# Moving a matmul's streamed weights 96 bytes into their buffers

## The chip, the cores and the metric

The kernel runs on one core of one Trainium2 chip. The metric is device time in microseconds (us) of one execution; lower is better. Before the change the median of three runs is 2471.81 us (2471.71 to 2472.35).

## The reference

The reference is a decoder trunk of two layers in float32, for one sequence of 256 tokens with 2,048 features. Cut to what matters here:

```python
u = rms_norm(h, mix_norm[0])
q, f, i, g = split(u @ w_a_in, 4)            # 2048 x 8192; i are the values
h = h + (norm(linear_attention(q, f, i)) * silu(g)) @ w_a_out
h = h + square(relu(rms_norm(h) @ w_mlp_up[0])) @ w_mlp_down[0]      # 2048 x 8192 x 2048
h = h + (p[0] @ w_ple_up[0]) * sigmoid(rms_norm(h) @ w_ple_gate[0])
k, v, f_logit = split(rms_norm(h) @ w_kvf)   # 2048 x (2048 + 2048 + 16)
dcum = cumsum(log_sigmoid(f_logit + b_f))
q = rms_norm(h, mix_norm[1]) @ w_b_q
h = h + softmax(q k^T / sqrt(128) + dcum_t - dcum_s, causal) v @ w_b_out
# then MLP and gate of layer 1, and a last rms_norm
```

## The kernel before, in words

**Splitting.** Every large product is made of float32r matmuls on split operands. A weight or an activation x becomes hi, its rounding to float32r, and lo = x - hi. A product is hi x hi + hi x lo + lo x hi, three matmuls that add up in PSUM.

**Loading weights.** `load_slab` (L79) loads a slab of up to 128 x 2,048 float32 weights by one DMA on SP's queue into `raw` (three buffers of 8,192 bytes a partition), or in parts. For each part (two as a rule) it takes a buffer `whi` and a buffer `wlo` of 1,024 elements (four buffers of each, in turn, 4,096 bytes a partition). ACT copies `raw` to `whi` (L93), DVE writes raw - whi to `wlo` (L94). So a slab fills two of the four buffers of each kind while the two before are in use.

**Feature-major products.** `mm_tile` (L98) makes 128 output features of all 256 tokens: for each of 16 chunks k of the input features, `mm_split` (L103) issues three matmuls (L112 to L114) whose stationary operand is a 128 x 128 block of `whi` or `wlo` and whose moving operand is 256 columns of the activation, `act[:, k, 0 or 1, :]`. Most of the kernel is made of these: the HGRN inputs, the output projections, both MLPs, the gates, keys and queries. The small products with `pt` (`ple`) take the same way.

**Token-major products.** `mm_tokens` (L118) makes 512 or 416 output features of all tokens, with tokens on the partitions. The roles are exchanged: the stationary operand is a 128 x 128 block of the activation, and the moving operand is the weight. Four slabs q hold four chunks of `cols` columns each. For each chunk and each half t of the tokens there are three matmuls (L131 to L133): activation hi x `whi`, activation hi x `wlo`, activation lo x `whi`. Thus one call has 4 x 4 x 2 x 3 = 96 matmuls. It is called four times with 512 columns for the values of layer 0 (`values`, one call before each fourth head, the first of them while x and the first weights are still being loaded, in smaller parts), and five times with 416 columns for the values and forget logits of layer 1 (the loop that fills `vv`).

**Where activations lie.** Split activations have a buffer of 16 x 2 x 256 elements and 64 more. `shifted` (L69) puts the data some elements into that buffer: 60 elements (240 bytes) in slots A and B, 28 (112 bytes) in slot C and for `pt`.

**Forget rows.** In the attention of layer 1, `cumulate` writes the negated running sums to `nd`, 16 x 256, and a DMA on POOL's queue stores them in a DRAM row buffer `dcum`. For each head `softmax` loads one row, broadcast to 128 partitions, into `ns` (two buffers, in turn), also on POOL's queue. `nd` has a buffer of its own.

**Order.** The order within each engine comes from the tile framework's scheduler and the program text. The framework places the buffers of a pool one after the other; the pool of `raw`, `whi` and `wlo` lies ahead of the pools that are opened later.

Of the kernel before, what the change touches and what calls it, by code (L numbers as in the profile page):

```python
# [10 lines left out]
F32 = mybir.dt.float32  # L11
F32R = mybir.dt.float32r
U32 = mybir.dt.uint32
AF = mybir.ActivationFunctionType
ALU = mybir.AluOpType
# [3 lines left out]
P = 128  # L19
T = 256  # L20
# [3 lines left out]
NH = 16  # L24
# [10 lines left out]
def yoco_kernel(ctx, tc, a, out):  # L35
    nc = tc.nc
    big = ctx.enter_context(tc.tile_pool(name="big", bufs=1))
    base = ctx.enter_context(tc.tile_pool(name="base", bufs=1))
    wp = ctx.enter_context(tc.tile_pool(name="wp", bufs=1))
# [36 lines left out]
        return shifted(big, KC, name, "slot" + which, 60)  # L76


    def load_slab(src, n, parts, before=None):  # L79

        raw = wp.tile([P, D], F32, name="raw", tag="raw", bufs=3)
        m = n // parts
        if not before:
            nc.sync.dma_start(raw[:, :n], src)
        got = []
        for i in range(parts):
            r = raw[:, i * m : (i + 1) * m]
            if before:
                before[i]()
                nc.sync.dma_start(r, src[:, i * m : (i + 1) * m])  # L90
            hi = wp.tile([P, 1024], F32R, name="whi", tag="whi", bufs=4)
            lo = wp.tile([P, 1024], F32R, name="wlo", tag="wlo", bufs=4)
            nc.scalar.copy(hi[:, :m], r)  # L93
            nc.vector.tensor_tensor(lo[:, :m], r, hi[:, :m].bitcast(F32), op=ALU.subtract)  # L94
            got.append((hi, lo))
        return got

# [3 lines left out]
    def mm_tile(src, act, kcs=KC):  # L101

        pairs = load_slab(src, kcs * P, 2 if kcs > 8 else 1)  # L103
        return mm_split(pairs, act, kcs)
# [12 lines left out]
    def mm_tokens(src, act, cols, before=None, after=None):  # L117

        pst = [psm.tile([P, 512], F32, name=f"pst{t}", tag="mm") for t in range(2)]
        for q in range(4):  # L120
            bef = before(q) if before else None
            parts = len(bef) if bef else 2
            pairs = load_slab(src(q), 4 * cols, parts, bef)
            for k in range(4):
                kk, m = 4 * q + k, 4 // parts
                hi, lo = (x[:, k % m * cols : (k % m + 1) * cols] for x in pairs[k // m])
                st, sp = kk == 0, kk == KC - 1
                for t in range(2):
                    o = pst[t][:, :cols]
                    tok = slice(t * P, (t + 1) * P)  # L130
                    nc.tensor.matmul(o, act[:, kk, 0, tok], hi, start=st, stop=False)  # L131
                    nc.tensor.matmul(o, act[:, kk, 0, tok], lo, start=False, stop=False)  # L132
                    nc.tensor.matmul(o, act[:, kk, 1, tok], hi, start=False, stop=sp)  # L133
            if after:
                after(q)
        return pst
# [96 lines left out]
    def ple(layer, u, stats, after, pool):  # L233

        praw = pool.tile([P, 2, T], F32, name="praw", tag="praw", bufs=1)
        nc.gpsimd.dma_start(praw, a["pT"][layer])
        pt = shifted(pool, 2, "pt", "pt", 28)
        for k in range(2):
            plain_split(pt, k, praw[:, k, :])
        rstd = None  # L240
        wu = None
        for n in range(KC):
            if n % 8 == 0:
                wu = load_slab(a["w_pu"][layer, n // 8], D, 2)
            pu = mm_split(wu, pt, kcs=2, off=2 * (n % 8))
            up = pool.tile([P, T], F32, name="up", tag="up", bufs=2)
            nc.scalar.copy(up, pu)
            last = layer == 1 and n == KC - 1
            ps = mm_tile(a["w_pg"][layer, n], u)
            rstd = rstd or stats.rstd()  # L250
            t = pool.tile([P, T], F32, name="gate", tag="gate", bufs=2)
            nc.vector.tensor_tensor(t, ps, rstd, op=ALU.mult)
            s = pool.tile([P, T], F32, name="sig", tag="sig", bufs=2)
            nc.scalar.activation(s, t, AF.Sigmoid)
            if last:

                nc.scalar.activation(scrap, s[:, 0:1], AF.Sqrt)
            nc.vector.tensor_tensor(up, up, s, op=ALU.mult)
            nc.vector.tensor_tensor(h[:, n, :], h[:, n, :], up, op=ALU.add)
            after(n)  # L260
# [18 lines left out]
    with tc.tile_pool(name="hg", bufs=2) as hp, tc.tile_pool(name="hps", bufs=1, space=PSUM) as hps:  # L279
# [60 lines left out]
        def values(grp):  # L340
            if grp == 0:
                return mm_tokens(lambda q: a["w_av"][0, q], u_a, 512,
                                 lambda q: [load_x(k, 1) for k in range(4)] if q == 0 else [load_x(4 * q), load_x(4 * q + 2)],
                                 lambda q: [stats.add(k) for k in range(4 * q, 4 * q + 4)])
            return mm_tokens(lambda q: a["w_av"][grp, q], u_a, 512)
# [226 lines left out]
    with tc.tile_pool(name="at", bufs=2) as ap, tc.tile_pool(name="aps", bufs=1, space=PSUM) as aps:  # L572
# [11 lines left out]
        for g in range(5):  # L584
            pv = mm_tokens(lambda q: a["w_vf"][g, q], u_kv, VC)
            if g == 0:
                norm["f"], norm["t"] = st_kv.rstd_both(aps, "pn")
            for t in range(2):
                nc.scalar.activation(vv[:, t, g * VC : (g + 1) * VC], pv[t][:, :VC], AF.Copy, scale=norm["t"][:, t : t + 1])
# [10 lines left out]
        nc.vector.tensor_scalar(ls, fl, 0.0, None, op0=ALU.min)  # L600
        nc.vector.tensor_tensor(ls, ls, fa, op=ALU.subtract)
        dt_ = ap.tile([P, 2, NH], F32, name="dt_", bufs=1)
        nd = ap.tile([NH, T], F32, name="nd", bufs=1)
        rows = dram.tile([NH, T], F32, name="dcum", tag="dcum")

        def cumulate():
# [169 lines left out]
```

## Time and profile before

| what | value |
|---|---|
| median of three runs | 2471.81 us |
| time of the profiled execution | 2472.09 us |
| its span, first to last instruction | 2470.0 us |
| mean granted TensorE clock | 0.998 |
| matmul records on PE | 20,808 |
| DVE busy, ACT busy | 1568.3 us, 1286.1 us |
| HBM read | 464.35 MB, 189 GB/s over the span |

How to read the profile: PE is the matmul engine, PEld its weight loads, DVE the vector engine, ACT the scalar engine, POOL the general one, SP the queue that issues the weight DMAs. A row such as "L112 PE MATMUL ps<-u_m,whi 128x256" names the line of the kernel, the engine, the output and the inputs, and the moving operand's shape. The length of a matmul in a row overlaps its neighbours, because matmuls are pipelined; the distance between the starts of two matmuls, in the timeline, is the pace. A float32 matmul that is not float32r appears as two records.

### The profile page before, as it was taken

The page shows a single profiled execution, that of the slowest core. Times are in us where ns is not written, and L with a number is a line of the kernel's source. Part 1 is how long each engine was busy: PE and PEld are TensorE (multiplying, and loading weights), DVE is VectorE, ACT ScalarE, POOL GpSimd, SP SyncE. Part 2 cuts the span into 40 slices and gives each one's busy share as a digit, 9 for nine tenths or more (in the row PEclk, how much of TensorE's full clock was granted, in tenths as well). Part 3 has the DMA queues.
Part 4 walks back from the last instruction along what each step waited for, and adds up shares of the span by engine and source line. Part 5 has one row for each costly group of instructions (what it writes and reads, how often), then busy time and mean ns, then how long its engine had stood idle before and what let it go on. Part 6 is the DMA issues. An engine that isn't in the chain of part 4 may idle for free.

```text
span 2470.0 us, 48653 instructions
## 1 busy us (share of the span) xinstructions
PE 2453.6 (99%) x20808; PEld 2431.0 (98%) x20808; DVE 1568.3 (63%) x2350; ACT 1286.1 (52%) x1966; POOL 23.1 (1%) x71
## 2 busy tenths in 40 slices
PE   9999999999999999999999999999999999999997
PEld 8999999999999999999999999999999999999997
DVE  8787797665555555556774566666555555555666
ACT  7666575555435435445664554555543443544564
POOL 1000000000000000000000000000000000000000
PEclk9999999999999999999999999999999999999999
DMA  7455445555555555555555655555555555555553
GB/s 256 172 180 181 184 167 203 201 189 190 201 190 192 201 188 194 199 188 195 197 179 185 198 180 171 181 196 188 195 198 189 197 196 190 197 194 190 199 192 120
DMA packets 68506, 469.62 MB, mean 190 GB/s; under 512 B 7937, under 2 KB 8641, under 8 KB 15041
## 3 DMA queue, kind: packets, MB, share of 16 engines
q1 hardware_dynamic: 66096, 460.88, 53.6%
q0 software_dynamic: 1760, 4.78, 1.0%
q8 instruction: 163, 2.67, 0.4%
q10 hardware_dynamic: 432, 0.85, 0.1%
q14 instruction: 55, 0.44, 0.0%
HBM read 464.35 MB, written 2.13 MB: 189 GB/s over the span
## 4 chain that ended last, share of the span: by engine, by line
PE 99%; DVE 0%; ACT 0%; DMA 0%; issue 0%; SPq 0%; DVEq 0%
PE ps L114 30%; PE ps L112 30%; PE ps L113 30%; PE pst L132 2%; PE pst L133 2%; PE pst L131 2%; PE pa L438 0%; PE pl L639 0%; PE ptp L662 0%; DMA h<-in_xT 0%; DVE h L709 0%; PE po L459 0%; PE ms L475 0%; PE pb L442 0%; PE pob L672 0%; PE pob L673 0%
## 5 line engine op out<-in xcount | busy, mean ns | idle before, releaser
L94 DVE TENSOR_TENSOR wlo<-raw,whi 128x1024 fp32r<-128x1024 f32 (+2 forms) x882 | 1069.2, 1213 | 674.2 <-ACT whi L93 673.4
L93 ACT CAST whi<-raw 128x1024 fp32r<-128x1024 f32 (+2 forms) x882 | 920.0, 1044 | 1083.4 <-PE ps L113 940.9
L112 PE MATMUL ps<-u_m,whi 128*128 128x256 f32 x2048 | 563.6, 275 | 0.0
L114 PE MATMUL ps<-u_m,wlo 128*128 128x256 f32 x2048 | 563.3, 275 | 0.0
L113 PE MATMUL ps<-u_m,whi 128*128 128x256 f32 x2048 | 563.3, 275 | 0.0
L112 PE MATMUL ps<-hid,whi 128*128 128x256 f32 x2048 | 563.2, 275 | 0.0
L113 PE MATMUL ps<-hid,whi 128*128 128x256 f32 x2048 | 563.2, 275 | 0.0
L114 PE MATMUL ps<-hid,wlo 128*128 128x256 f32 x2048 | 563.2, 275 | 0.0
L112 PEld LDWEIGHTS ps<-u_m,whi 128*128 128x128 f32 x2048 | 384.5, 188 | 0.1
L113 PEld LDWEIGHTS ps<-u_m,whi 128*128 128x128 f32 x2048 | 384.5, 188 | 0.1
L114 PEld LDWEIGHTS ps<-u_m,wlo 128*128 128x128 f32 x2048 | 384.4, 188 | 0.0
L112 PEld LDWEIGHTS ps<-hid,whi 128*128 128x128 f32 x2048 | 384.4, 188 | 0.0
L113 PEld LDWEIGHTS ps<-hid,whi 128*128 128x128 f32 x2048 | 384.4, 188 | 0.0
L114 PEld LDWEIGHTS ps<-hid,wlo 128*128 128x128 f32 x2048 | 384.4, 188 | 0.0
L112 PE MATMUL ps<-u_a,whi 128*128 128x256 f32 x768 | 214.0, 279 | 0.0
L114 PE MATMUL ps<-u_a,wlo 128*128 128x256 f32 x768 | 213.1, 277 | 0.0
L113 PE MATMUL ps<-u_a,whi 128*128 128x256 f32 x768 | 212.3, 276 | 0.0
L112 PEld LDWEIGHTS ps<-u_a,whi 128*128 128x128 f32 x768 | 144.3, 188 | 0.2
L113 PEld LDWEIGHTS ps<-u_a,whi 128*128 128x128 f32 x768 | 144.3, 188 | 0.2
L114 PEld LDWEIGHTS ps<-u_a,wlo 128*128 128x128 f32 x768 | 144.3, 188 | 0.0
L112 PE MATMUL ps<-u_p,whi 128*128 128x256 f32 x512 | 140.8, 275 | 0.0
L113 PE MATMUL ps<-u_p,whi 128*128 128x256 f32 x512 | 140.7, 275 | 0.0
(257 smaller groups left out, 3659.8 us busy)
## 6 DMA issues: line engine op xcount, KB each, us to landing
raw<-in_w_up SPq DMA_DIRECT2D x128, 1024.0 KB, 4.8
raw<-in_w_down SPq DMA_DIRECT2D x128, 1024.0 KB, 4.8
raw<-in_w_ain SPq DMA_DIRECT2D x48, 1024.0 KB, 4.8
raw<-in_w_pg SPq DMA_DIRECT2D x32, 1024.0 KB, 4.8
raw<-in_w_vf SPq DMA_DIRECT2D x20, 832.0 KB, 4.4
raw<-in_w_aout SPq DMA_DIRECT2D x16, 1024.0 KB, 4.7
raw<-in_w_k SPq DMA_DIRECT2D x16, 1024.0 KB, 4.8
raw<-in_w_q SPq DMA_DIRECT2D x16, 1024.0 KB, 6.3
```

What stands on the lines that cost most here:

```text
L93: nc.scalar.copy(hi[:, :m], r)
L94: nc.vector.tensor_tensor(lo[:, :m], r, hi[:, :m].bitcast(F32), op=ALU.subtract)
L112: nc.tensor.matmul(ps, wk(pair, kl, 0), act[:, k, 0, :], start=st, stop=False)
L113: nc.tensor.matmul(ps, wk(pair, kl, 0), act[:, k, 1, :], start=False, stop=False)
L114: nc.tensor.matmul(ps, wk(pair, kl, 1), act[:, k, 0, :], start=False, stop=sp)
L131: nc.tensor.matmul(o, act[:, kk, 0, tok], hi, start=st, stop=False)
L132: nc.tensor.matmul(o, act[:, kk, 0, tok], lo, start=False, stop=False)
L133: nc.tensor.matmul(o, act[:, kk, 1, tok], hi, start=False, stop=sp)
```

## The change

The buffers of `whi` and `wlo` get 32 elements (128 bytes) more each. `load_slab` takes a `shift`, 0 unless given, and uses the elements from `shift` on. `mm_tokens` passes 24, so that its weights lie 96 bytes into their buffers; `mm_tile` and the slabs of `ple` pass nothing, and their weights stay at the start. The eight buffers together take 1,024 bytes a partition more. `nd`, which took 1,024 bytes, now shares the two buffers of `ns`.

```diff
-    def load_slab(src, n, parts, before=None):
+    def load_slab(src, n, parts, before=None, shift=0):
...
-            hi = wp.tile([P, 1024], F32R, name="whi", tag="whi", bufs=4)
-            lo = wp.tile([P, 1024], F32R, name="wlo", tag="wlo", bufs=4)
-            nc.scalar.copy(hi[:, :m], r)
-            nc.vector.tensor_tensor(lo[:, :m], r, hi[:, :m].bitcast(F32), op=ALU.subtract)
+            hi = wp.tile([P, 1024 + 32], F32R, name="whi", tag="whi", bufs=4)[:, shift : shift + m]
+            lo = wp.tile([P, 1024 + 32], F32R, name="wlo", tag="wlo", bufs=4)[:, shift : shift + m]
+            nc.scalar.copy(hi, r)
+            nc.vector.tensor_tensor(lo, r, hi.bitcast(F32), op=ALU.subtract)
             got.append((hi, lo))
...
-            pairs = load_slab(src(q), 4 * cols, parts, bef)
+
+            pairs = load_slab(src(q), 4 * cols, parts, bef, 24)
...
-        nd = ap.tile([NH, T], F32, name="nd", bufs=1)
+        nd = ap.tile([NH, T], F32, name="nd", tag="ns", bufs=2)
```

## The prediction

> **What bounds the kernel now.** I read the page first: busy times, slices, chain. Then I read the groups kept apart by shape, for the instructions that the change touches, and then the timeline of PE, because the groups give the length of one matmul and not the distance from one to the next.
>
> ```profile
> span 2470.0 us, 48653 instructions
> PE 2453.6 (99%) x20808; PEld 2431.0 (98%) x20808; DVE 1568.3 (63%) x2350; ACT 1286.1 (52%) x1966; POOL 23.1 (1%) x71
> ...
> PE 99%; DVE 0%; ACT 0%; DMA 0%; issue 0%; SPq 0%; DVEq 0%
> PE ps L114 30%; PE ps L112 30%; PE ps L113 30%; PE pst L132 2%; PE pst L133 2%; PE pst L131 2%; PE pa L438 0%; PE pl L639 0%; PE ptp L662 0%; DMA h<-in_xT 0%; DVE h L709 0%; PE po L459 0%; PE ms L475 0%; PE pb L442 0%; PE pob L672 0%; PE pob L673 0%
> ```
>
> PE is the chain: 99% of the span. The three lines of the feature-major products hold 90% of it, and the three lines of the token-major products, L131 to L133, hold some 6%. The change can save time only where matmuls follow each other more closely.
>
> ```profile
> L131 PE MATMUL pst<-whi,u_kv 128*128 128x416 f32 x160 | 56.2, 351 | 0.0
> L132 PE MATMUL pst<-wlo,u_a 128*128 128x512 f32 x128 | 51.0, 398 | 1.1 <-DVE wlo L94 1.1
> L133 PE MATMUL pst<-whi,u_a 128*128 128x512 f32 x128 | 50.4, 394 | 0.0
> L131 PE MATMUL pst<-whi,u_a 128*128 128x512 f32 x128 | 49.4, 399 | 0.8 <-ACT whi L93 0.8
> ```
>
> There are 3 x 128 = 384 token-major matmuls of 512 columns (the values, four groups of 96) and 3 x 160 = 480 of 416 columns (five groups of 96). Their idle time is 1.9 us in all, so nearly all their time is pace. The 351 and 394 ns are lengths that overlap the neighbours. The pace is in the starts:
>
> ```profile
> 99.72 0.39 PE L133 MATMUL pst<-whi,u_a 128*128 128x512 f32 x1
> ...
> 101.82 0.39 PE L133 MATMUL pst<-whi,u_a 128*128 128x512 f32 x1
> ```
>
> ```profile
> 1278.70 0.35 PE L131 MATMUL pst<-whi,u_kv 128*128 128x416 f32 x1
> ...
> 1279.82 0.35 PE L131 MATMUL pst<-whi,u_kv 128*128 128x416 f32 x1
> ...
> 1280.95 0.35 PE L131 MATMUL pst<-whi,u_kv 128*128 128x416 f32 x1
> ```
>
> ```profile
> 1999.80 0.28 PE L114 MATMUL ps<-u_m,wlo 128*128 128x256 f32 x1
> ...
> 2000.93 0.28 PE L112 MATMUL ps<-u_m,whi 128*128 128x256 f32 x1
> ```
>
> Nine steps take 2.10 us with 512 columns, 0.2333 each. With 416 columns a chunk of six steps takes 1.12 and the next 1.13 us, 0.1875 each. Ten steps take 1.13 us with 256 columns, 0.113 each. By columns alone, 512 would take twice the 256, 0.2267, and 416 would take 0.1842: the token-major products are 6.6 and 3.3 ns a matmul slower than that.
>
> **Where the operands lie.** In the feature-major products the weights are stationary and start at byte 0 of whi or wlo, in steps of 512 bytes. The activation moves, 60 or 28 elements (240 or 112 bytes) into its buffer, in steps of 1,024 bytes. All these buffers begin at multiples of 128 bytes in the program. So modulo 128 the weight lies at 0 and the moving operand at 112, which is 16 bytes short of the weight's place. In the token-major products the roles are exchanged: the stationary activation lies at 112, the moving weight at 0, 16 bytes past it. After the change the moving weight lies at 96, again 16 bytes short (its steps, 2,048 and 1,664 bytes, are multiples of 128). That is the reason to expect the pace of the other products, and nothing more than a likeness.
>
> **The change part by part.** *The pace.* What would an undisturbed pass of 512 columns take? The f32 matmuls of the attention give a near row, since one f32 column takes about twice the time of one of the columns here. The timeline merges the two records of such a matmul, and the view of line 639 has the length of one (least, median, most):
>
> ```profile
> 1411.61 0.60 PE L639 MATMUL pl<-ksb,qsb 128*128 128x256 f32 x2
> ```
>
> ```profile
> L639 PE MATMUL pl<-ksb,qsb x32: 379/380/382, 1387.0 to 1572.6; 128*128 128x256 f32 x32
> ```
>
> Two records of L639 cover 0.60 us and each is 0.38 long, so the second starts 0.22 after the first. That is 256 f32 columns, against 0.113 for 256 of the kind used here: nearly double. I take 0.220 for 512 columns, and for 416 the point between, 0.1133 + 160/256 x (0.220 - 0.1133) = 0.180. The upper end is the plain proportion above, 0.2267 and 0.1842. That the 256-column pace need not scale is seen here:
>
> ```profile
> 1374.33 0.29 PE L608 MATMUL pd<-ls,tri 128*128 128x16 f32 x2
> 1374.47 0.38 PE L609 MATMUL pd<-ls,ones 128*128 128x16 f32 x2
> 1374.69 0.37 PE L610 MATMUL pd<-ls,tri 128*128 128x16 f32 x2
> 1374.99 0.39 PE L613 MATMUL pr<-tri,ls 128*16 128x128 f32 x2
> ```
>
> Six records with 16 columns fill 0.66 us, 0.11 each. Each brings its own weights, so a weight load seems to set a floor of about 0.11 whatever the columns, and the 0.113 of 256 columns stands almost on it. Part of that 0.113 is the load's and need not double.
>
> The Trainium skill, "TensorE: Matmul & The Clock Gate", section "Wait — 56ns, not 53.3ns?", gives a start-to-start of N / 2.4 GHz plus about 2.5 ns for a warm array. By that estimate 512 columns take 215.8 ns and 416 take 175.8, from which the trace differs by 17.5 and 11.7 ns; the sum below would by that be 288 x 17.5 + 480 x 11.7 ns = 10.7 us.
>
> *How many of them pay.* The table by stretches gives, after the stretch and its length, the busy time of PE, PEld, DVE, ACT and POOL, then the clock, the DMA share and GB/s:
>
> ```profile
> 14.50:30.60 16.10, 16.10 (x69) 12.95 (x70) 15.89 (x28) 13.87 (x25) 0.00 (x0) 1.00 0.95 338
> 86.50:108.00 21.50, 21.50 (x111) 17.98 (x110) 10.39 (x13) 9.92 (x12) 0.00 (x0) 1.00 0.50 187
> ...
> 1299.00:1368.00 69.00, 69.00 (x368) 68.61 (x367) 32.67 (x32) 31.95 (x39) 0.00 (x0) 1.00 0.56 195
> ```
>
> The clock is granted in full (1.00) in all of them. In the later value groups and in the attention's groups PE never waits, DVE and ACT are under half busy and the DMA engines at 0.50 to 0.56: a faster PE finds its weights. That is 3 x 96 = 288 matmuls of 512 columns and all 480 of 416. In the first value group DVE is busy for 15.89 of 16.10 us and the DMA engines for 0.95; the 69 matmuls there run at 0.233 now, but any faster they would wait for wlo. I count them at nothing, and at 69 x 13.3 ns = 0.9 us for the far end.
>
> Sum: 288 x (233.3 - 220.0) ns = 3.8 us, and 480 x (187.5 - 180.0) ns = 3.6 us, together 7.4 us. Lower end by the proportion: 288 x 6.6 + 480 x 3.3 ns = 1.9 + 1.6 = 3.5 us.
>
> *The writes at byte 96.* ACT and DVE now write whi and wlo 96 bytes in. The near rows are DVE's writes 112 or 240 bytes into hid against those at the start of o2s:
>
> ```profile
> L188 DVE TENSOR_TENSOR hid<-hsq,hid 128x256 fp32r<-128x256 f32 x128 | 53.7, 419 | 0.0
> L188 DVE TENSOR_TENSOR o2s<-o,o2s 128x256 fp32r<-128x256 f32 x16 | 6.7, 416 | 0.0
> ```
>
> They take 419 and 416 ns. At 1% it costs nothing, because both engines have half their time free; in the first group, where they have not, 1% of 16 us would be 0.2 us.
>
> *The 128 bytes more.* Eight buffers grow, 1,024 bytes in all, so whatever lies behind them moves by a multiple of 1,024 and keeps its place modulo 128. The memory comes from nd.
>
> *nd takes a buffer of ns.* nd is written once and read by one DMA:
>
> ```profile
> L617 POOL DMA_DIRECT2D dcum<-nd x1: 517/517/517, 1376.5 to 1376.5; - x1
> ...
> DMA to landing us min/median/max: 1.7/1.7/1.7
> ```
>
> The first ns load already waits for that DMA, since it reads what it wrote. The second load would reuse nd's buffer, one head later, and wait for a read that landed at about 1378. POOL's queue holds only these sixteen loads. Cost: nothing, with a whole head as cover; without it the second load would start some 1.7 us late, which half a head hides.
>
> The program's own time in the profiled execution was 2472.09 us, 2.1 over its span; the median is 2471.81. From the median: 2471.8 - 7.4 = 2464.4 us.
>
> **The rivals.** *It does nothing.* The place of the operands does not matter, and 0.233 and 0.188 are what such lengths cost when every matmul brings its own weights. For it: both paces are steady. Against it: between them lie 45.8 ns for 96 columns, 0.48 ns a column, steeper than the 0.42 from 0.113 to 0.220, so something beyond a fixed start and the columns is paid. Time 2471.8 us. The Trainium skill, the same page, section "Step-by-step: what each phase is for", says that PE reads the streamed operand and the next weights through two independent ports, so that the load takes nothing from the running matmul; by that the places could not disturb each other, and no run here yet shows it either way.
>
> *Half of it.* The pace of 256 columns scales with the columns, and the change only removes what lies over that line: 3.5 us, 2468.3 us. Only the 0.11 floor speaks against it.
>
> *More of it.* The 0.60 and 0.38 us above are rounded, and 0.215 fits them as well as 0.220; 416 columns would then take 0.1133 + 160/256 x 0.1017 = 0.1769. With the first value group gaining too, that is 357 x 18.3 + 480 x 10.6 ns = 11.6 us, 2460.2 us.
>
> *Slower: the other products pay.* A buffer of 4,224 bytes puts every second buffer of whi and wlo at 128 modulo 256, where all stood at 0. A feature-major tile of 16 chunks splits its weights over two buffers, so half its weight loads move. The kernel has 400 such tiles (48 for the HGRN inputs, 256 for the MLPs, 32 for the gates, 16 each for both output projections, keys and queries) with 48 matmuls each; half is 9,600. If they went at the pace of the one such matmul whose operands stand otherwise (o2s moves from 64 modulo 128, mselr, its weight, stands at 32 to 44),
>
> ```profile
> 64.89 0.29 PE L475 MATMUL ms<-o2s,mselr 128*128 128x256 f32 x1
> 65.01 0.29 PE L113 MATMUL ps<-u_a,whi 128*128 128x256 f32 x1
> ```
>
> ```profile
> 373.05 0.39 PE L475 MATMUL ms<-o2s,mselr 128*128 128x256 f32 x2
> 373.28 0.29 PE L112 MATMUL ps<-u_a,whi 128*128 128x256 f32 x1
> ```
>
> which is 0.12 and 0.115 from start to start (the second row holds two), some 4.2 ns over 0.1133, they would cost 40.3 us: 2471.8 - 7.4 + 40.3 = 2504.7 us. It decides from 7.4 us / 9,600 = 0.8 ns a matmul on. Against it: with 416 columns the moving operand stands at 0 and at 128 modulo 256 in turn, chunk by chunk, and two chunks in turn take 1.12 and 1.13 us.
>
> **How the numbers follow.** The forecast has 0.44, more of it 0.08, half of it 0.16, nothing 0.20, slower 0.12. A difference under 0.2%, 4.9 us, is about what a measurement here can tell from none. Faster by over 0.2% takes the forecast and more of it, 0.52; within 0.2% half and nothing, 0.36; slower 0.12. The range runs from just below more of it, 2459.5, to just above nothing, 2473.0; it leaves out the slower case, 0.12, and the edges.
>
> **What would show it.** Right: in the timeline L131 to L133 start 0.220 apart with 512 columns and 0.180 with 416; the groups shrink (a value group of 96 from 22.4 to 21.1 us, an attention group from 18.0 to 17.3); L112 to L114 stay at 0.113; DVE and ACT groups keep their means. Half: 0.227 and 0.184. Nothing: starts unchanged. Slower: L112 to L114 at 0.115 or more, and in pairs of eight chunks. New idle time before L132, put down to wlo, in the first value group would say that its 69 matmuls cannot go faster. The forecast is wrong if the token-major pace does not move, or if the other products' does.

## The result and the profile after

The change makes the kernel slower: 2517.45 us (median of four runs, 2517.1 to 2517.53) against 2471.82 us, a ratio of 1.0183 with a 95% interval of 1.017 to 1.0196. That is 45.6 us more.

Two lines of the page of before, for the weights that DVE writes and for one group of feature-major matmuls:

```profile
L94 DVE TENSOR_TENSOR wlo<-raw,whi 128x1024 fp32r<-128x1024 f32 (+2 forms) x882 | 1069.2, 1213 | 674.2 <-ACT whi L93 673.4
L112 PE MATMUL ps<-u_m,whi 128*128 128x256 f32 x2048 | 563.6, 275 | 0.0
```

The page of the changed kernel, whose line numbers are higher by one here:

```profile
span 2515.4 us, 48653 instructions
PE 2499.5 (99%) x20808; PEld 2476.3 (98%) x20808; DVE 1569.2 (62%) x2350; ACT 1283.5 (51%) x1966; POOL 23.3 (1%) x71
...
L95 DVE TENSOR_TENSOR wlo<-raw,whi 128x1024 fp32r<-128x1024 f32 (+2 forms) x882 | 1069.4, 1213 | 691.1 <-ACT whi L94 689.8
L113 PE MATMUL ps<-u_m,whi 128*128 128x256 f32 x2048 | 569.4, 278 | 0.0
```

The instructions are as many as before, and DVE and ACT are as busy; DVE's writes of wlo take 1,213 ns in the mean, as they did. Only PE is busy longer, and not by waiting. A feature-major matmul, whose code the change does not touch, is 278 ns long instead of 275. The pace shows in a count of starts inside the first MLP. The table by stretches for PE alone (stretch, its length, busy time and instructions, clock, DMA share, GB/s), before:

```profile
500.00:1100.00 600.00, 600.00 (x5297) 1.00 0.56 194
```

and after:

```profile
500.00:1100.00 600.00, 600.00 (x5188) 1.00 0.55 190
```

A stretch also counts the two or three matmuls that are under way at its start. Less 2.4 of them, PE starts 5,295 matmuls in 600 us before and 5,186 after, 113.3 and 115.7 ns each, with the full clock in both. There are 400 feature-major tiles of 48 matmuls and 192 matmuls with `pt`, together 19,392; 19,392 x 2.4 ns = 47 us. Summed from start to start over the two traces, the feature-major products take 44.7 us more, the 416-column products 0.9 more and the 512-column products 0.3 less. That is the loss of 45.6 us, within the rounding.

It is not spread evenly. The traces hold no addresses; the places of buffers in this text are those that the program gives them. In the first MLP a tile's first eight chunks come from one buffer and its last eight from the next, 128 bytes off. The timeline of PE after the change, at the start of a tile, at its ninth chunk and at the next tile:

```profile
577.64 0.28 PE L113 MATMUL ps<-u_m,whi 128*128 128x256 f32 x1
...
580.38 0.28 PE L113 MATMUL ps<-u_m,whi 128*128 128x256 f32 x1
...
583.20 0.28 PE L113 MATMUL ps<-u_m,whi 128*128 128x256 f32 x1
```

The first 24 steps (distances from one start to the next) take 2.74 us, 114.2 ns each, the other 24 take 2.82 us, 117.5. In the second MLP whole tiles alternate instead, by their pace (presumably because `ple` holds two of the four buffers over eight tiles and so changes their order), and the fast ones show how the pace comes back:

```profile
1999.17 0.28 PE L113 MATMUL ps<-u_m,whi 128*128 128x256 f32 x1
...
2000.60 0.28 PE L113 MATMUL ps<-u_m,whi 128*128 128x256 f32 x1
...
2004.00 0.28 PE L113 MATMUL ps<-u_m,whi 128*128 128x256 f32 x1
...
2006.67 0.28 PE L115 MATMUL ps<-u_m,wlo 128*128 128x256 f32 x1
...
2009.25 0.28 PE L113 MATMUL ps<-u_m,whi 128*128 128x256 f32 x1
```

The tile begins at 1999.17. Its first twelve steps take 1.43 us (119 ns each), the next thirty 3.40 us (113.3 each). The last two rows lie in the next tile, from the other buffers: 22 steps in 2.58 us, 117.3 ns each. So half of the matmuls lose 4 ns throughout, and the other half lose some at each switch: with a mean of 115.7 in the first MLP they are at 2 x 115.7 - 117.3 = 114.1.

The token-major products, for which the change was made, gain nothing. After the change, with 512 and with 416 columns:

```profile
95.72 0.39 PE L133 MATMUL pst<-whi,u_a 128*128 128x512 f32 x1
...
98.98 0.40 PE L135 MATMUL pst<-whi,u_a 128*128 128x512 f32 x1
```

```profile
1302.74 0.35 PE L133 MATMUL pst<-whi,u_kv 128*128 128x416 f32 x1
...
1303.88 0.35 PE L133 MATMUL pst<-whi,u_kv 128*128 128x416 f32 x1
...
1305.05 0.35 PE L133 MATMUL pst<-whi,u_kv 128*128 128x416 f32 x1
```

Fourteen steps in 3.26 us are 0.2329 with 512 columns (0.2333 before). With 416 columns six steps take 1.14 and the next six 1.17 us, 0.190 and 0.195 (0.1875 before).

### The profile page after: what moved, and what is told of

Its sections match the earlier page's. It is cut to its first block, busy times and chain, and to the rows that moved or that the text cites. A ratio compares the mean times of both kernels' runs of the same rounds, so it can differ in the third digit from the quotient of the medians.

```text
span 2515.4 us, 48653 instructions
## 1 busy us (share of the span) xinstructions
PE 2499.5 (99%) x20808; PEld 2476.3 (98%) x20808; DVE 1569.2 (62%) x2350; ACT 1283.5 (51%) x1966; POOL 23.3 (1%) x71
## 4 chain that ended last, share of the span: by engine, by line
PE 99%; DVE 0%; DMA 0%; ACT 0%; issue 0%; SPq 0%; DVEq 0%
PE ps L113 30%; PE ps L114 30%; PE ps L115 30%; PE pst L134 2%; PE pst L135 2%; PE pst L133 2%; PE pa L440 0%; PE pl L641 0%; DMA raw<-in_w_av 0%; PE ptp L664 0%; DVE h L711 0%; PE ms L477 0%; PE pb L444 0%; PE pob L675 0%; PE pb L443 0%; PE po L462 0%
## 5 line engine op out<-in xcount | busy, mean ns | idle before, releaser
L95 DVE TENSOR_TENSOR wlo<-raw,whi 128x1024 fp32r<-128x1024 f32 (+2 forms) x882 | 1069.4, 1213 | 691.1 <-ACT whi L94 689.8
L113 PE MATMUL ps<-u_m,whi 128*128 128x256 f32 x2048 | 569.4, 278 | 0.0
L113 PE MATMUL ps<-hid,whi 128*128 128x256 f32 x2048 | 569.0, 278 | 0.0
L114 PE MATMUL ps<-hid,whi 128*128 128x256 f32 x2048 | 569.0, 278 | 0.0
L114 PE MATMUL ps<-u_m,whi 128*128 128x256 f32 x2048 | 569.0, 278 | 0.0
```

The source lines that it names most:

```text
L95: nc.vector.tensor_tensor(lo, r, hi.bitcast(F32), op=ALU.subtract)
L113: nc.tensor.matmul(ps, wk(pair, kl, 0), act[:, k, 0, :], start=st, stop=False)
L114: nc.tensor.matmul(ps, wk(pair, kl, 0), act[:, k, 1, :], start=False, stop=False)
```

## The experiments

Theory A: the pace of a float32r matmul depends on the moving operand's place minus the stationary one's, modulo 256 bytes; "difference" stands for that below. The kernel before has the difference 112 in all feature-major products; the buffers of 4,224 bytes make it 240 for half of them. The rivals: the shift or the writes at byte 96 cost the time (B), or a weight that does not begin at a multiple of 256 bytes is slow to load, whatever moves (C).

**The buffers alone.**

```diff
-            pairs = load_slab(src(q), 4 * cols, parts, bef, 24)
+            pairs = load_slab(src(q), 4 * cols, parts, bef, 0)
```

> The buffers of whi and wlo keep their 128 bytes more, but every weight starts at byte 0 of its buffer (shift 0). Theory A: the pace of a feature-major matmul depends on how the stationary weight and the moving activation lie to each other modulo 256 bytes; the longer buffers put every second weight buffer at 128 modulo 256, and that is the whole loss. Then this kernel is as slow as the changed one: about 2517 us, L113 to L115 at 113.3 ns from the even buffers and about 117.3 from the odd ones, and the 512-column pace back at 233. Theory B: the 96-byte place of the token-major weights, or writing them there, costs the time: about 2472 us, and 113.3 ns throughout.

It took 2515.05 us (ratio 1.0173, 1.0158 to 1.0189), 43.1 us more than the 2471.96 us beside it. The MLP's count is that of the changed kernel:

```profile
500.00:1100.00 600.00, 600.00 (x5188) 1.00 0.56 190
```

The 128 bytes more in each buffer are the loss, all but 2.4 us of it, with no weight shifted. Those 2.4 us lie in the token-major products: summed from start to start, the 512-column ones take 1.7 us more with the shift and the 416-column ones 1.0 more. The expectation of 0.233 for 512 columns held for half of the chunks alone:

```profile
99.48 0.39 PE L133 MATMUL pst<-whi,u_a 128*128 128x512 f32 x1
...
100.88 0.39 PE L133 MATMUL pst<-whi,u_a 128*128 128x512 f32 x1
...
102.25 0.39 PE L133 MATMUL pst<-whi,u_a 128*128 128x512 f32 x1
```

A chunk of six steps takes 1.40 us (0.233 each), and one from the next buffer 1.37 (0.228).

**The shift alone.** Buffers of 1,024 elements, and 24 elements of shift only where `cols` is 416; nd shares ns.

```diff
-            hi = wp.tile([P, 1024 + 32], F32R, ...)[:, shift : shift + m]
+            hi = wp.tile([P, 1024], F32R, ...)[:, shift : shift + m]
...
+            pairs = load_slab(src(q), 4 * cols, parts, bef, 24 if cols == VC else 0)
```

> The buffers keep 4,096 bytes; only the 416-column products, whose parts fill 3,328 bytes, lie 96 bytes in. The 512-column products stay at 0. nd shares ns as in the change. Theory A: feature-major pace 113.3 ns everywhere; in the 416-column products the chunks at 96 modulo 256 go at about 193 ns and those at 224 at about 188, as they do in the changed kernel, so 240 matmuls x 5 ns = 1.2 us are lost: about 2473 us. Theory B (the shift costs the time): five of the nine token-major calls carry it, so about 25 of the 45.6 us: 2497 us.

It took 2472.81 us against 2471.96, ratio 1.0004 (0.9994 to 1.0013): theory B falls, and nd in ns's buffers costs nothing to see. Its timeline shows the chunks at 96 and at 224 modulo 256:

```profile
1303.21 0.35 PE L133 MATMUL pst<-whi,u_kv 128*128 128x416 f32 x1
...
1304.37 0.35 PE L133 MATMUL pst<-whi,u_kv 128*128 128x416 f32 x1
...
1305.50 0.35 PE L133 MATMUL pst<-whi,u_kv 128*128 128x416 f32 x1
```

Six steps take 1.16 us (193 ns) and the next six 1.13 (188): the shift slows one chunk in two.

**256 bytes more instead of 128.** `sq`, which holds the squares for a norm, gives the memory.

```diff
-            hi = wp.tile([P, 1024 + 32], F32R, ...)[:, shift : shift + m]
+            hi = wp.tile([P, 1024 + 64], F32R, ...)[:, shift : shift + m]
...
-                sq = base.tile([P, T], F32, name="sq", tag="sq", bufs=2)
+                sq = base.tile([P, T], F32, name="sq", tag="sq", bufs=1)
```

> As the changed kernel, with all its shifts, but the buffers get 256 bytes more instead of 128, so every buffer of whi and wlo starts at a multiple of 256 again. The memory comes from sq, which has one buffer instead of two. Theory A: about 2473 us (2471.8 + 1.2 for the 416-column chunks at 96 modulo 256), and 113.3 ns for every feature-major matmul. Theory B (shift, or unaligned writes by ACT and DVE): about 2517 us, like the changed kernel. If larger buffers as such cost time: over 2517 us.

It took 2475.13 us against 2471.96, ratio 1.0014 (1.0004 to 1.0024). The MLP is back at its pace with larger buffers and every shift in place:

```profile
500.00:1100.00 600.00, 600.00 (x5296) 1.00 0.57 194
```

The 512-column weights have the difference 240 throughout here, and yet two paces, in the second and in the third value group:

```profile
99.63 0.39 PE L133 MATMUL pst<-whi,u_a 128*128 128x512 f32 x1
...
101.97 0.40 PE L134 MATMUL pst<-wlo,u_a 128*128 128x512 f32 x1
```

```profile
189.63 0.39 PE L134 MATMUL pst<-wlo,u_a 128*128 128x512 f32 x1
...
191.89 0.39 PE L135 MATMUL pst<-whi,u_a 128*128 128x512 f32 x1
```

Ten steps take 2.34 us in the one and 2.26 in the other, with the same places. What chose the pace there, no run shows.

The 2 us over the expectation are those of the single sq:

> The kernel before with one buffer of sq instead of two, which the runs with larger buffers needed. If the second buffer only lets ACT run ahead of DVE under PE's cover, 2472 us; if it is what the run with 256 bytes more lost, some 2 us more, 2474 us.

That kernel, the one before with one buffer of sq, took 2475.99 us against 2471.92 (1.0017, 1.0008 to 1.0026), 4.1 us more. PE has a wait there that the kernel before lacks:

```profile
PE ps L112 <- ACT v L352: 2.7, 1, 2.7
```

So beside its own base the run with 256 bytes more is 0.9 us faster, not slower.

**The activation moved, no weight.**

```diff
-        return shifted(big, KC, name, "slot" + which, 60)
+        return shifted(big, KC, name, "slot" + which, 28)
```

> The kernel before with one number changed: activations in slots A and B lie 28 elements into their buffers instead of 60, that is 128 bytes earlier. No weight moves. Theory A (the two operands' places to each other modulo 256): the feature-major matmuls that read A or B, 13,056 of 19,392, go at about 117.3 ns instead of 113.3: 52 us more, about 2524 us; those that read slot C stay at 113.3. Theory C (a weight is slow to load when it does not start at a multiple of 256 bytes, whatever the activation): all weights stand where they stood, about 2472 us.

It took 2515.83 us (1.0177, 1.0162 to 1.0192), 43.9 us more. In the output projection of layer 0, which reads slot B, the stretch from 400 to 470 us holds 620 matmuls in the kernel before and 600 in this one:

```profile
400.00:470.00 70.00, 70.00 (x620) 1.00 0.56 197
```

```profile
400.00:470.00 70.00, 70.00 (x600) 1.00 0.53 186
```

Less 2.4 each, that is 117.1 against 113.3 ns, with every weight where it was before. Theory C falls: the same weight is fast or slow by where the activation lies. The total came out 8 us under the expectation, which counted the fast pace of before for every matmul (it is not held everywhere, see below) and left the 512-column products alone, whose activation moved too. Summed from start to start, those products take 2.6 us less than before, and the feature-major products of `u_a` lose 6.6 us where 9.2 were counted; that is 5.2 of the 8 us.

**Everything moved by 128, and everything at 240.** A tile of 128 bytes ahead of the weight buffers puts all of them at 128 modulo 256. In the first kernel all activations move along; in the second all stay at 112. Both have one sq.

```diff
+    pad128 = ctile([P, 32], "pad128")
+    nc.gpsimd.memset(pad128, 0.0)
...
-        return shifted(big, KC, name, "slot" + which, 60)
+        return shifted(big, KC, name, "slot" + which, 28)    # first kernel only
...
-        return shifted(late, KC, name, "slotC", 28)
+        return shifted(late, KC, name, "slotC", 60)          # second kernel only, pt likewise
```

> Every operand of the feature-major products moves by 128 modulo 256: 128 bytes of padding ahead of the weight buffers put all of them at 128, and the activations in A and B lie 28 elements in instead of 60, so that all activations stand at 240. The difference stays 112. sq has one buffer. Theory A: 113.3 ns throughout, about 2472 to 2475 us. If the absolute place counts (weights at 128, or activations at 240): 117.3 ns throughout, about 2472 + 19,392 x 4 ns = 2549 us.

> The suspected cost doubled: all weight buffers at 128 modulo 256, as in the run before, and all activations at 112 as in the kernel before, so that every feature-major matmul has the difference 240 that half of them have in the changed kernel. sq has one buffer. Theory A: 117.3 ns throughout, 19,392 x 4 ns = 77 us more, about 2549 us. If the loss comes from places that alternate between one buffer and the next and not from the difference 240: about 2472 to 2475 us.

They took 2476.11 us (1.0016, 1.0007 to 1.0026) and 2543.07 us (1.0287, 1.0273 to 1.0301). Against the base with one sq, 2475.99, that is 0.1 and 67.1 us. The MLP, first kernel and then second:

```profile
500.00:1100.00 600.00, 600.00 (x5296) 1.00 0.56 194
```

```profile
500.00:1100.00 600.00, 600.00 (x5124) 1.00 0.55 188
```

Absolute places do not matter, their difference does, and the loss needs no alternation: with 240 throughout, each matmul takes 600 us / 5,122 = 117.1 ns. Doubling the share of such matmuls did not double the 43 us of the first run, which fits the timeline above: a kernel that alternates also pays at each switch between the kinds of buffer.

**A map.** The shift grows by 16 bytes from one group of four tiles, or one token-major slab, to the next; the 416-column chunks stand 448 columns apart. The buffers have 256 bytes more, and sq is single.

```diff
+        s = count["f"] // 4 % 16 * 4
+        count["f"] += 1
+        pairs = load_slab(src, kcs * P, 2 if kcs > 8 else 1, None, s)
```

> A map of the pace over the place of the weights. Buffers of whi and wlo with 256 bytes more (all at multiples of 256), sq with one buffer. The weights of each four feature-major tiles in turn lie 0, 16, 32 up to 240 bytes into their buffers, and the weights of each token-major slab in turn likewise; the 416-column chunks stand 448 columns apart, so that all chunks of a slab have one place modulo 256. Theory A: the feature-major pace depends on moving minus stationary place modulo 256: 113.3 ns with 112 (weights at byte 0), about 117.3 with 240 (weights at byte 128), and the other fourteen places fall between 112 and 118. With 512 columns about 227 ns at byte 96 and 233 at byte 0, with 416 columns about 193 at byte 96 and 188 at byte 224. Theory C (only the weight's own place counts in the load): every place but byte 0 is slow in the feature-major products, and the moving operand's place changes nothing in the token-major ones.

It took 2557.81 us, in one run. In the first MLP each place of the weights has 18 us in this table; shown are bytes 0, 16, 176 and 240:

```profile
499.00:517.00 18.00, 18.00 (x159) 1.00 0.54 182
522.00:540.00 18.00, 18.00 (x152) 1.00 0.55 183
...
750.00:768.00 18.00, 18.00 (x162) 1.00 0.59 200
...
839.00:857.00 18.00, 18.00 (x152) 1.00 0.55 183
```

Less 2.4, these are 115, 120, 113 and 120 ns, where one matmul more or less is 0.8 ns. The other twelve places have 152 to 157 matmuls, 116 to 120 ns, some of them over the 118 that I expected at most. Byte 176 (difference 192) is as fast as byte 0 (difference 112) was in the kernel before; I had expected only one such place. Byte 0 itself falls short here, at 159, because the MLP's f32 matmul lies in its stretch, at 501.96 us; of that more below. With 512 columns the map is another: byte 96 (difference 240) goes at 0.227, as expected, though 240 is slow with 256 columns, and with 416 too (0.193).

**The second fast place, held.** Activations 16 elements in (A, B) and 48 (C, pt), so that all have the difference 192, and the 512-column products 64.

```diff
-        return shifted(big, KC, name, "slot" + which, 60)
+        return shifted(big, KC, name, "slot" + which, 16)
...
-        return shifted(late, KC, name, "slotC", 28)
+        return shifted(late, KC, name, "slotC", 48)
```

> The kernel before with three numbers changed, and no weight and no buffer: activations lie 16 elements in (slots A and B) or 48 (slot C and pt), so that all stand at 192 modulo 256. Theory A with the map: feature-major difference 192 goes at 113.5 ns like 112; the 512-column products then have moving minus stationary 64 and go at 227 instead of 233.3, 357 x 6.3 ns = 2.2 us less; the 416-column chunks have 64 and 192 in turn, 189.4 instead of 188.4, 0.5 us more. Together 2470.2 us. If the map's second fast place holds only for that weight place and not for the difference: 2472 + 19,392 x 4 ns = about 2549 us.

> As the run before, and the 416-column chunks stand 448 columns apart, 208 bytes into buffers of the old size, so that all have moving minus stationary 16 modulo 256. Theory A with the map: 512 columns at 227 ns (2.2 us less than before the change), 416 columns at 186.7 (480 x 1.7 ns = 0.8 us less): about 2468.9 us. If spread chunks make ACT or DVE slower so that PE waits: over 2470 us.

They took 2527.56 us (1.0224, 1.021 to 1.0238) and 2525.57 us (1.0216, 1.0202 to 1.023). Both expectations failed. The first of the two, by stretches:

```profile
400.00:470.00 70.00, 70.00 (x620) 1.00 0.57 196
500.00:1100.00 600.00, 600.00 (x5096) 1.00 0.54 187
```

The output projection runs at the fast pace, 113.3 ns, and the MLP behind it at 117.8, with the same difference. The switch is in its timeline, at the f32 matmul L160 that sums the squares for the norm:

```profile
485.67 0.28 PE L112 MATMUL ps<-u_m,whi 128*128 128x256 f32 x1
...
487.25 0.28 PE L114 MATMUL ps<-u_m,wlo 128*128 128x256 f32 x1
487.37 0.59 PE L160 MATMUL ps_ssq<-ssq,ones 128*128 128x256 f32 x2
...
488.04 0.28 PE L114 MATMUL ps<-u_m,wlo 128*128 128x256 f32 x1
...
489.92 0.28 PE L112 MATMUL ps<-u_m,whi 128*128 128x256 f32 x1
```

Fourteen steps take 1.58 us ahead of the f32 matmul L160, 112.9 ns each, and sixteen take 1.88 us behind it, 117.5 (starts are given to 10 ns). The slow pace then lasts through the MLP, for over 700 us, until behind the next f32 matmul of that line the fast one is back:

```profile
1212.13 0.60 PE L160 MATMUL ps_ssq<-ssq,ones 128*128 128x256 f32 x2
...
1213.27 0.28 PE L112 MATMUL ps<-u_p,whi 128*128 128x256 f32 x1
...
1214.41 0.28 PE L113 MATMUL ps<-u_p,whi 128*128 128x256 f32 x1
```

Ten steps take 1.14 us there. The second MLP repeats the first: 5,097 matmuls in 600 us. The kernel before has the same f32 matmul, and recovers:

```profile
488.14 0.28 PE L113 MATMUL ps<-u_m,whi 128*128 128x256 f32 x1
...
489.69 0.28 PE L113 MATMUL ps<-u_m,whi 128*128 128x256 f32 x1
...
492.64 0.28 PE L113 MATMUL ps<-u_m,whi 128*128 128x256 f32 x1
```

Thirteen steps take 1.55 us (119 ns), the next 26 take 2.95 us (113.5). So the difference alone does not give the pace. With 192 two paces hold themselves, and what ran before chooses. With 112, in the kernel before, PE came back each time: from the 17th feature-major matmul behind one of another kind on, all but 6 of 18,049 steps are under 116 ns. Theory A stands with this addition. The spread chunks of the second kernel took 2.0 us off the first.

**The change without its loss.** hi and lo share one buffer of 2,112 elements, so that four buffers grow by 256 bytes instead of eight by 128; the 416-column chunks stand 448 columns apart, 128 bytes in; 512 columns lie 96 bytes in, or in the second kernel 224.

```diff
+            both = wp.tile([P, 2048 + 64], F32R, name="whl", tag="whl", bufs=4)
+            hi, lo = (both[:, j * 1024 + shift :] for j in range(2))
...
+            pairs = load_slab(src(q), 4 * cols, parts, bef, 32 if step else 24, step)
```

> The change without its loss: hi and lo of a slab part share one buffer of 2,112 elements (four of them, 1,024 bytes more in all, as much as nd gives), so that every weight block at shift 0 stands at a multiple of 256. Activations stay where they were, difference 112. The 512-column weights lie 96 bytes in, the 416-column chunks stand 448 columns apart, 128 bytes in. Theory A with the map: feature-major 113.3 to 113.5 ns; 512 columns at 227 to 228.5 instead of 233.3 (357 x 4.8 to 6.3 ns = 1.7 to 2.2 us); 416 columns at 186.7 instead of 188.4 (0.8 us): 2469.0 to 2469.5 us. If a shared buffer makes ACT or PE wait for DVE: over 2472 us.

> As the run before, with the 512-column weights 224 bytes in instead of 96, so that their difference is 112, the one at which the feature-major products keep their fast pace. Theory A with the map: 512 columns at 226.6 ns, 357 x 6.7 ns = 2.4 us less, 0.8 us less for 416 columns: 2468.8 us. If places that the map shows fast go slower when held for a whole call, as the difference 192 did: up to 2471.5 us.

They took 2469.70 us (0.9991, 0.9982 to 1.0) and 2470.54 us (0.9994, 0.9986 to 1.0003) against 2471.99. The first one's third value group, whose pace the second group shares:

```profile
189.62 0.39 PE L139 MATMUL pst<-whl,u_a 128*128 128x512 f32 x1
...
191.88 0.39 PE L140 MATMUL pst<-whl,u_a 128*128 128x512 f32 x1
```

Ten steps take 2.26 us, 0.226 each. In the second kernel the second value group stays at 0.233 (nine steps in 2.10 us), as in the run with 256 bytes more; its expectation had named that case, up to 2471.5 us. The first kernel's 2.3 us less is the gain that was in the change: 0.1%, at the edge of what the runs can tell from none.

## Why the prediction was wrong, point by point

**The step that failed** is "The 128 bytes more": it speaks of what lies behind the eight buffers, which "keeps its place modulo 128", and charges nothing for the buffers themselves, every second of which moves by 128. The period is 256. Measured, this step costs 43.1 us (the buffers alone) of the 53.1 between the forecast of 2464.4 and the result; 7.4 more are the gain that did not come. The text of the kernel before held the clue, and I passed it by: slots A and B shift by 60 elements and slot C by 28, a difference of 128 bytes, and in the program A and B begin at 128 modulo 256 while C begins at 0. Both shifts lead to 112 modulo 256; modulo 128 there would have been no reason for two numbers.

**Where the operands lie.** The likeness was false for the same reason. 96 minus 112 is 240 modulo 256, a slow difference of the other products, and not their 112. Nor do the products share their fast places: with 512 columns 240 was held at 0.226 in the run with shared buffers.

**The rival that came true** was "Slower: the other products pay", with its place right (every second buffer at 128 modulo 256) and a chance of 0.12. Its price of 4.2 ns for half was 4.0 for that half (117.3 against 113.3). What it left out is the other half, 0.8 ns each for recovering after a switch: 9,696 x (4.0 + 0.8) = 46.5 us, against the 40.3 that I had and the 44.7 of the traces. The pairs of eight chunks that it named are there in the first MLP. The evidence that I set against it, two chunks in turn of 1.12 and 1.13 us with the moving operand at 0 and 128, held only for those differences (144 and 16); with 240 and 112 the run with the shift alone shows 193 and 188 ns.

**The pace.** 0.220 and 0.180 were not reached by any place that a run held. The best held for a stretch was 0.226 to 0.227 with 512 columns, which is the plain proportion (0.2267) of the rival "Half of it"; with 416 columns it was 0.1867, above the 0.1842 of that line. The f32 passes were the wrong neighbour. In the changed kernel 512 columns stayed at 0.233, with 240 and 112 in turn, though each of the two was held at 0.227 in another run. The Trainium skill, "TensorE: Matmul & The Clock Gate", section "Wait — 56ns, not 53.3ns?", would give 215.8 ns there, an estimate from its formula. The runs here stay 10 ns above it.

**The ports.** The Trainium skill, the same page, section "Step-by-step: what each phase is for", has the streamed operand and the next weights read through two independent ports, with no cost to the running matmul. Here moving the activation by 128 bytes, and nothing else, changed 113.3 to 117.1 ns. The measurement decides: the pace depends on the two places together. That the two reads disturb each other is the likeliest reading, but no run shows it, nor where in the chip they would meet.

**How many pay; the writes at byte 96; nd.** No new wait of PE in the later groups, DVE and ACT means unchanged, 2472.81 us with nd in ns's buffers: these steps held.

## What to carry to other kernels

A buffer's length is a change to every later buffer's address: before padding one, list each operand's place modulo 256 in the pairs that meet in a matmul, also for the products that are not edited. Where two shifts in a kernel look arbitrary, work out what they have in common before choosing a period. And a place that is fast for one tile is not yet fast: hold it for a stage, with the f32 matmuls that come between, and measure each matmul shape for itself.

## What was not expected of the hardware

A float32r matmul of 256 columns has a pace of 113.3 to about 120 ns by the difference of its operands' places, at a full granted clock and with no wait in the profile. At one difference (192) it has two paces, 113.3 and 117.8 ns, and a single f32 matmul switched it for over 700 us. With 512 columns 240 has two as well, 0.226 and 0.234 us. And in a kernel in which PE is busy for 99%, one small buffer less (sq) cost 4.1 us.
